# Wide products without a reader in the opening, an earlier first load of modulation tiles, and a fifth raw slot

## The chip, the cores and the metric

The kernel runs on one core of one Trainium2 chip. Its time is the device time of one execution in microseconds (us), from launch to end; the table below gives the median of three runs. The engines are TensorE (PE in the rows; its weight loads are PEld), VectorE (DVE), ScalarE (ACT), GpSimd (POOL) and SyncE (SP), whose queue issues almost all transfers.

## The reference, cut to what matters

Two transformer layers work on a sequence of 512 tokens with 1024 features, in fp32. Each layer modulates a normalised input, projects it, runs four kinds of attention heads side by side, and then a feed-forward block:

```python
c_act = jax.nn.silu(c)
for l in range(DEPTH):
    mod = c_act @ w_ada[l] + b_ada[l]
    sh1, sc1, g1, sh2, sc2, g2 = [t[:, None, :] for t in jnp.split(mod, N_ADA, axis=-1)]
    h = rmsnorm(x, norm_mix_g[l]) * (1.0 + sc1) + sh1
    z = h @ w_in[l]
    ...
    x = x + g1 * (o @ w_out[l])
    h = rmsnorm(x, norm_mlp_g[l]) * (1.0 + sc2) + sh2
    x = x + g2 * (jnp.square(jax.nn.relu(h @ w_up[l])) @ w_down[l])
```

So before the first projection of layer 0 can start, the squares of x must be summed over the features, a reciprocal root taken, and two of the six modulation vectors (the scale, part 1, and the shift, part 0) worked out from 8 MB of `w_ada`.

## The kernel before

Everything lies transposed: features on 128 partitions, eight tiles of features (k = 0 to 7), 512 tokens as columns. A product in fp32 accuracy is made of three products of rounded halves (`hi` and `lo` of the activations, `whi` and `wlo` of the weights). For each weight tile the class `Weights` takes a slot of the pool `rawp` (four slots of 512 KB, given out in turn, shared with later modulation tiles `adaw`), loads it on SP's queue, has ACT copy it to `whi` (L87) and POOL subtract that to `wlo` (two instructions, L91). A slot is free again when both have read it. Nearly all PE work after the opening is such products (`pj`, `px`).

The opening is `start` (L1148). SP's queue issues x (six transfers), two weight tiles, and then in the order of the code one pair of modulation tiles per k (`ada0`, part 1 ahead of part 0, four slots of a pair) with the other weight tiles between. PE first spreads c over all partitions (`cbP`, eight fp32 products of 128 columns). ACT and DVE square and add the eight tiles of x; PE sums the result over the partitions (`nsum`, four products of one column); DVE and POOL make the reciprocal root (`rsv`, `rs`); PE spreads it (`rsb`). For each k DVE then makes the two modulation columns from the pair of tiles (L191, a product with a sum over 1024 columns each) and the normalised tile `ht` (L1196), ACT makes `hi` (L1199), and POOL or DVE `lo`. Five weight tiles (`n` = 5) are worked on at the same time: with each k come three groups of five products (L1223): hi by whi, the earlier lo by whi, and a hi two back by wlo; the last 30 products are a section of their own. That is 120 products in the opening. The banks `pt` of the pool `psT` are two.

The order of instructions on each engine is fixed when the program is built, by a scheduler that works with its own estimate of times; `tc.issue_after` keeps an instruction behind a named one. Each SP transfer carries one of eight completion semaphores in turn (DMAHW0 to DMAHW7 in the rows), so a transfer waits for the one eight places ahead of it to have landed.

After the opening come the projections and heads of layer 0's attention: `mlas` (12 groups of one-column sums), the scores `sc`, ACT's exponentials `e` (L601), POOL's or DVE's scaling of `e` (L573), PE's transposes `pt` (L626), ACT's and DVE's halves `ph` and `pl` of them (L448, L449), and PE's products `po` (L641, L642), with projections of later heads between.

Of the kernel before, what the change touches and what calls it, by code (L numbers as in the profile page):

```python
# [10 lines left out]
F32 = mybir.dt.float32  # L11
# [6 lines left out]
P = 128  # L18
# [4 lines left out]
AHEAD = (1, 3, 2, 1, 0, 0)  # L23
LAHEAD = (2, 3, 2, 1, 0, 0)
PRELOAD = 2
NSPLIT = 3
KPOOL = 5
NJ0 = 1
# [3 lines left out]
NQ = S // P  # L32
# [77 lines left out]
def layer_stack(ctx: ExitStack, tc: tile.TileContext, a, out):  # L110
    nc = tc.nc
    cons = ctx.enter_context(tc.tile_pool(name="cons", bufs=1))
    rawp = ctx.enter_context(tc.tile_pool(name="rawp", bufs=4))
    hlp = ctx.enter_context(tc.tile_pool(name="hlp", bufs=4))
    hsp = ctx.enter_context(tc.tile_pool(name="hsp", bufs=16))
    smp = ctx.enter_context(tc.tile_pool(name="smp", bufs=2))
# [3 lines left out]
    psT = ctx.enter_context(tc.tile_pool(name="psT", bufs=2, space=PSUM))  # L120
# [3 lines left out]
    def mmbank(name):  # L124
        return psA.tile([P, 512], F32, tag="mm", name=name)

    def tmp_tile(name):
        return wkp.tile([P, S], F32, tag="tmp", name=name, bufs=4)
# [3 lines left out]
    X = {}  # L132
# [3 lines left out]
    ident = cons.tile([P, P], F32, name="ident")  # L136
# [15 lines left out]
    def load_consts():  # L152
        nc.sync.dma_start(cs, a["cs"])
        nc.sync.dma_start(maskL, a["maskL"])
        nc.sync.dma_start(cbias, a["cbias"])
        nc.sync.dma_start(cmask, a["cmask"])
        nc.sync.dma_start(bmask, a["bmask"])
        nc.sync.dma_start(csum, a["csum"])

    def load_x(src, queue):  # L160

        v = xp.tile([P, KT // 2, S], F32, tag="V", name="x")
        tiles = [v[:, k, :] for k in range(KT // 2)]
        for k in (0, 2):
            queue.dma_start(v[:, k : k + 2, :], src[:, k : k + 2, :])
        for k in range(KT // 2, KT):
            tiles.append(xp.tile([P, S], F32, tag="KL", name="x", bufs=4))
            queue.dma_start(tiles[k], src[:, k, :])
        X["x"] = tiles
# [3 lines left out]
    cv = vecs[:, OFF_C : OFF_C + KT]  # L173
# [11 lines left out]
    W = Weights(nc, rawp, hlp, 3, 3)  # L185


    def ada_cols(w, l, part, m, cv=cb):

        off = l * VL + OFF_BADA + 8 * part + m  # L190
        last["ada"] = nc.vector.tensor_tensor_reduce(  # L191
            out=w, in0=cv, in1=w, scale=1.0, scalar=vecs[:, off : off + 1],
            op0=ALU.mult, op1=ALU.add, accum_out=mod[l][:, part, m : m + 1],
        )

    def ada_start(pool, m, cv):

        raw = pool.tile([P, 2, 1024], F32, tag="ada0", name="ada0", bufs=4)
        for part in (1, 0):
            nc.sync.dma_start(raw[:, part, :], a["wadaP"][m, :, part, :])  # L200
            ada_cols(raw[:, part, :], 0, part, m, cv)

    ada_todo = [(0, part, m) for part in (2, 4, 3, 5) for m in range(KT)]
    ada_todo += [(1, part, m) for part in (1, 0, 2, 4, 3, 5) for m in range(KT)]
# [1 line left out]
    last = {}  # L206
# [42 lines left out]
    def rstd_cols(ps, n, scale_cols):  # L249

        v = smp.tile([P, 8], F32, tag="rsv", name="rsv")
        for c0, c1, sc in scale_cols:
            nc.vector.tensor_scalar(  # L253
                v[:, c0:c1], ps[:, c0:c1], sc, EPS, op0=ALU.mult, op1=ALU.add
            )
        r = smp.tile([P, 8], F32, tag="rs", name="rs")
        last["pow"] = nc.gpsimd.tensor_tensor(r[:, 0:n], v[:, 0:n], mhalf[:, 0:n], op=ALU.pow)  # L257
        return r

    def bcast_cols(ps, r, c0, n):  # L260

        for j in range(n):
            nc.tensor.matmul(  # L263
                ps[:, j * P : (j + 1) * P],
                r[:, c0 + j : c0 + j + 1].to_broadcast([P, P]), ident,
                start=True, stop=True,
            )

    def sbank(name):
        return psS.tile([P, 512], F32, tag="sc", name=name)  # L270
# [44 lines left out]
    def h_tiles(pool, tag, bufs):  # L315
        return [
            tuple(pool.tile([P, S], F32R, tag=tag, name=f"h{x}", bufs=bufs) for x in ("hi", "lo"))
            for _ in range(KT)
        ]
# [828 lines left out]
    def start(pool, n):  # L1148


        nonlocal psS
        load_x(a["xT"], nc.sync)
        for _ in range(PRELOAD):
            W._load()
        cps = ctx.enter_context(ExitStack())
        psC = cps.enter_context(tc.tile_pool(name="psC", bufs=1, space=PSUM))
        cbP = psC.tile([P, D], F32, name="cbP")
        for k in range(KT):
            nc.tensor.matmul(
                cbP[:, k * P : (k + 1) * P], cact[:, k : k + 1].to_broadcast([P, P]), ident,  # L1160
                start=True, stop=True,
            )
        acc = wkp.tile([P, S], F32, tag="sqacc", name="sqacc", bufs=1)
        nc.scalar.activation(acc, X["x"][0], AF.Square)
        for k in range(1, KT):
            sq = mmbank("sq")
            nc.scalar.activation(sq, X["x"][k], AF.Square)
            nc.vector.tensor_tensor(acc, acc, sq, op=ALU.add)
        rsb = psO.tile([P, 512], F32, tag="po", name="rsb0")
        ps = psT.tile([P, 512], F32, tag="pt", name="nsum")  # L1170
        for j in range(NQ):
            nc.tensor.matmul(
                ps[:, j : j + 1], acc[:, j * P : (j + 1) * P], ones, start=True, stop=True
            )
        r = rstd_cols(ps, NQ, [(0, NQ, 1.0 / D)])
        bcast_cols(rsb, r, 0, NQ)
        hs = h_tiles(hsp, "hs", 16)
        pss = [mmbank("pj") for _ in range(min(n, 3))]
        pss += [psT.tile([P, 512], F32, tag="pt", name="pj") for _ in range(min(n, 5) - 3)]
        W.other_pool.update({i: (pool, 4) for i in range(4)})  # L1180
        ws = []
        gs = smp.tile([P, KT], F32, tag="gs", name="gs")
        for k in range(KT):
            ada_start(pool, k, cbP)
            if k < n:
                W.split_ahead, W.load_ahead = AHEAD[k], LAHEAD[k]
                with tc.issue_after(last["pow"].ins):
                    ws.append(W.get())
            g = vecs[:, OFF_NMIX + k : OFF_NMIX + k + 1]
            nc.scalar.activation(  # L1190
                gs[:, k : k + 1], mod[0][:, 1, k : k + 1], AF.Identity, bias=g, scale=g
            )
            t = tmp_tile("ht")
            hi, lo = hs[k]
            with tc.issue_after(last["ada"].ins):
                last["dve"] = nc.vector.scalar_tensor_tensor(  # L1196
                    t, X["x"][k], gs[:, k : k + 1], rsb, op0=ALU.mult, op1=ALU.mult
                )
            nc.scalar.activation(hi, t, AF.Identity, bias=mod[0][:, 0, k : k + 1])  # L1199
            if k < KPOOL:  # L1200
                nc.scalar.activation(t, t, AF.Identity, bias=mod[0][:, 0, k : k + 1])
                nc.gpsimd.tensor_tensor(lo, t, hi.bitcast(F32), op=ALU.subtract)
            else:
                last["dve"] = nc.vector.scalar_tensor_tensor(
                    lo, t, mod[0][:, 0, k : k + 1], hi.bitcast(F32), op0=ALU.add, op1=ALU.subtract
                )
        for _ in range(NADA):
            i = ada_state["i"]
            raw = pool.tile([P, 2, 1024], F32, tag="ada0", name="ada0", bufs=4)
            nc.sync.dma_start(raw, a["wadaD"][i : i + 2].rearrange("t p r -> p t r"))  # L1210
            with tc.issue_after(last["dve"].ins):
                for j in range(2):
                    ada_cols(raw[:, j, :], *ada_todo[i + j], cbP)
            ada_state["i"] += 2
        W.split_ahead, W.load_ahead = 3, 3
        while W.n_split < n + NSPLIT:
            W._split()
        load_consts()
        nc.scalar.activation(cb, cbP, AF.Copy)
        cps.close()  # L1220
        psS = ctx.enter_context(tc.tile_pool(name="psS", bufs=2, space=PSUM))
        def part(g, w, k, h):
            nc.tensor.matmul(  # L1223
                pss[g], ws[g][w][:, k, :], hs[k][h], start=(k + w + h == 0),
                stop=(k == KT - 1 and w == 1),
            )


        for k in range(KT - 1):
            for w, j, h in ((0, k, 0), (0, k - 1, 1), (1, k - 2, 0)):  # L1230
                if j >= 0:
                    for g in range(n):
                        part(g, w, j, h)
        k = KT - 1
        for g in range(n):
            for w, j, h in (
                (0, k - 1, 1), (1, k - 2, 0), (1, k - 1, 0), (0, k, 0), (0, k, 1), (1, k, 0)
            ):
                part(g, w, j, h)
        return hs, pss  # L1240
# [152 lines left out]
```

## Time and profile before

| | |
|---|---|
| median of 3 runs | 1287.53 us (1287.36 to 1289.71) |
| the profiled execution: its own time | 1289.0 us |
| its span, first to last instruction | 1287.2 us |
| PE busy | 1245.9 us (97% of the span) |
| DVE, ACT, POOL busy | 681.3, 583.4, 545.8 us |
| mean granted clock of TensorE | 0.981 |

The profiled execution lies 1.5 us above the median, and its span 1.8 us below its own time. In the rows a line begins with its start in us and its length; "[3.77 <-POOL e L573]" is the idle time of the engine ahead of it and what ended that. "x5" is the number of instructions merged into a row; an fp32 product of PE is recorded as two. [...]

### The profile page before, as it was taken

To read this page: it belongs to the slowest core of one execution; us is meant where nothing else is said; L and a number is where in the kernel's file an instruction comes from. 1 tells how busy PE (TensorE), PEld (TensorE's weight loads), DVE (VectorE), ACT (ScalarE), POOL (GpSimd) and SP (SyncE) were. 2 spreads that over 40 slices of the span, in tenths; PEclk is the share of its full clock that TensorE was granted. 3 is DMA by queue.
4 is the path that set the end of the run, shared out by engine and by line. 5 is a ranking of instruction groups with operands and counts; after the bars stand their busy time and mean duration, and the time that the engine had idled before them with its cause. 6 is when DMAs were issued, how large, how long until landed. Compare 5 with 4: busy or idle time off the path is not lost. (4 is left out here: it accounts for less than half of the span.)

```text
span 1287.2 us, 17945 instructions
## 1 busy us (share of the span) xinstructions
PE 1245.9 (97%) x6572; PEld 1042.1 (81%) x6572; DVE 681.3 (53%) x1498; ACT 583.4 (45%) x1121; POOL 545.8 (42%) x495
## 2 busy tenths in 40 slices
PE   5989999989999999999999999999999999999997
PEld 4878787879888888888899778778988888888887
DVE  5758867976455554553255685895543223123124
ACT  5557767744442231331245675884443223223120
POOL 5423323454645445445425432334364444444430
PEclk7989999999999999999999999999999999999998
DMA  9645324452366756655334411313142233323312
GB/s 339 246 118 164 115 72 142 148 201 90 120 191 204 243 183 224 222 182 199 126 110 140 135 43 57 99 58 107 50 131 89 93 98 98 98 85 95 99 33 66
DMA packets 53128, 171.02 MB, mean 133 GB/s; under 512 B 6192, under 2 KB 9776, under 8 KB 53040
## 3 DMA queue, kind: packets, MB, share of 16 engines
q1 hardware_dynamic: 51312, 165.67, 39.5%
q10 hardware_dynamic: 1728, 4.20, 1.0%
q8 instruction: 52, 0.85, 0.3%
q14 instruction: 36, 0.29, 0.1%
HBM read 163.29 MB, written 4.19 MB: 130 GB/s over the span
## 5 line engine op out<-in xcount | busy, mean ns | idle before, releaser
L91 POOL TENSOR_TENSOR wlo<-raw,whi 128x512 fp32r<-128x512 f32 (+3 forms) x372 | 488.2, 1337 | 560.8 <-ACT whi L87 525.3
L87 ACT ACTIVATE whi<-raw 128x1024 fp32r<-128x1024 f32 (+3 forms) x186 | 193.8, 1046 | 459.2 <-PE px L368 249.0
L368 PE MATMUL pj<-hlo,whi 128*128 128x512 f32 (+1 forms) x768 | 288.0, 376 | 0.0
L367 PE MATMUL pj<-hhi,whi 128*128 128x512 f32 (+1 forms) x768 | 287.1, 376 | 0.0
L369 PE MATMUL pj<-hhi,wlo 128*128 128x512 f32 (+1 forms) x768 | 287.1, 374 | 0.0
L367 PE MATMUL px<-a,whi 128*128 128x512 f32 (+2 forms) x584 | 214.9, 368 | 0.0
L368 PE MATMUL px<-a,whi 128*128 128x512 f32 (+2 forms) x584 | 214.7, 368 | 0.0
L369 PE MATMUL px<-a,wlo 128*128 128x512 f32 (+2 forms) x584 | 214.6, 368 | 0.0
L411 DVE SCALAR_TENSOR_TENSOR x<-px,mod,x 128x512 f32<-128x512 f32 (+2 forms) x95 | 62.7, 665 | 199.2 <-PE px L369 199.2
L369 PEld LDWEIGHTS pj<-hhi,wlo 128*128 128x128 f32 x768 | 144.9, 189 | 26.7
L368 PEld LDWEIGHTS pj<-hlo,whi 128*128 128x128 f32 x768 | 145.1, 189 | 26.1
L367 PEld LDWEIGHTS pj<-hhi,whi 128*128 128x128 f32 x768 | 144.1, 188 | 26.1
L191 DVE CUSTOM_DVE_ANT_0 adaw<-cb,adaw,vecs 128x1024 f32<-128x1024 f32 x78 | 102.0, 1307 | 50.7 <-DMA adaw<-in_wadaD 50.7
L368 PEld LDWEIGHTS px<-a,whi 128*128 128x128 f32 x584 | 109.7, 188 | 19.7
L367 PEld LDWEIGHTS px<-a,whi 128*128 128x128 f32 x584 | 109.7, 188 | 19.7
L369 PEld LDWEIGHTS px<-a,wlo 128*128 128x128 f32 x584 | 109.7, 188 | 19.7
L1134 DVE SCALAR_TENSOR_TENSOR t<-pj,r 128x512 f32<-128x512 f32 x64 | 44.1, 691 | 148.0 <-ACT r L1133 147.8
L449 DVE TENSOR_TENSOR a<-t,a 128x512 fp32r<-128x512 f32 x64 | 81.8, 1280 | 41.9 <-ACT a L448 41.9
L601 ACT ACTIVATE e<-e,nm 128x128 f32<-128x128 f32 (+5 forms) x160 | 85.9, 539 | 10.3 <-DVE nm L596 9.8
L449 DVE TENSOR_TENSOR pl<-pt,ph 128x512 fp32r<-128x512 f32 (+1 forms) x112 | 64.8, 597 | 5.9 <-ACT ph L448 5.1
L626 PE MATMUL pt<-ident,e 128*128 128x128 f32 x376 | 60.9, 276 | 4.3 <-POOL e L573 3.8
L448 ACT ACTIVATE ph<-pt 128x512 fp32r<-128x512 f32 (+1 forms) x112 | 56.0, 524 | 13.5 <-PE pt L626 12.2
(237 smaller groups left out, 1806.6 us busy)
## 6 DMA issues: line engine op xcount, KB each, us to landing
adaw<-in_wadaD SPq DMA_DIRECT2D x78, 512.0 KB, 4.4
raw<-in_wup SPq DMA_DIRECT2D x64, 512.0 KB, 3.6
raw<-in_wdown SPq DMA_DIRECT2D x64, 512.0 KB, 3.5
raw<-in_winT SPq DMA_DIRECT2D x28, 512.0 KB, 3.8
ada<-in_wadaP SPq DMA_DIRECT2D x16, 512.0 KB, 8.9
raw<-in_wout SPq DMA_DIRECT2D x16, 512.0 KB, 3.5
cw<-in_cw SPq DMA_DIRECT2D x4, 512.0 KB, 5.0
raw<-in_cw SPq DMA_DIRECT2D x4, 512.0 KB, 4.8
```

The source lines that it names most:

```text
L87: self.nc.scalar.activation(vh[0:rows], raw[0:rows], AF.Copy)
L91: eng.tensor_tensor(lo[0:rows, c], flat[0:rows, c], hi[0:rows, c].bitcast(F32), op=ALU.subtract)
L191: last["ada"] = nc.vector.tensor_tensor_reduce(out=w, in0=cv, in1=w, scale=1.0, scalar=vecs[:, off : off + 1], op0=ALU.mult, op1=ALU.add, ...
L367: nc.tensor.matmul(ps, wh[:, k, :], hh[:, c], start=first, stop=False)
L368: nc.tensor.matmul(ps, wh[:, k, :], hl[:, c], start=False, stop=False)
L369: nc.tensor.matmul(ps, wl[:, k, :], hh[:, c], start=False, stop=last)
L411: last["dve"] = nc.vector.scalar_tensor_tensor(X["x"][m][:, c], ps, mod[l][:, part, m : m + 1], X["x"][m][:, c], op0=ALU.mult, op1=ALU.add)
L448: nc.scalar.activation(hi, src, AF.Copy)
L449: last["dve"] = nc.vector.tensor_tensor(lo, src, hi.bitcast(F32), op=ALU.subtract)
L601: nc.scalar.activation(ee, ee, AF.Exp, bias=nm[:, n : n + 1], scale=-1.0, accum_out=den[:, n : n + 1])
L626: nc.tensor.transpose(pt[:, c : c + P], p[n][:, col : col + P], ident)
L1134: nc.vector.scalar_tensor_tensor(t, ps, 0.0, r, op0=ALU.max, op1=ALU.mult)
```

## The change

Six things are edited. `WARM = (7, 2, 3)` gives the numbers of products `warm`: ident by a tile of x, 512 columns, into a bank `pt` that nobody reads. Seven stand on PE behind `cbP`, two behind `nsum`, three behind `rsb`, and `rsb` stands behind the two. `ada_start` now returns the DVE part as a function, so that the first pair of tiles is loaded ahead of the two weight tiles, and the first modulation column on DVE ahead of `rsv`, the second behind it. `rawp` has five slots. The scratch memory that the program keeps for transfers with addresses made on the chip is set to 8192 bytes.

```diff
+WARM = (7, 2, 3)
...
-    rawp = ctx.enter_context(tc.tile_pool(name="rawp", bufs=4))
+    rawp = ctx.enter_context(tc.tile_pool(name="rawp", bufs=5))
...
         for part in (1, 0):
             nc.sync.dma_start(raw[:, part, :], a["wadaP"][m, :, part, :])
-            ada_cols(raw[:, part, :], 0, part, m, cv)
+
+        def products(parts=(1, 0)):
+            for part in parts:
+                ada_cols(raw[:, part, :], 0, part, m, cv)
+        return products
...
         load_x(a["xT"], nc.sync)
-        for _ in range(PRELOAD):
-            W._load()
         cps = ctx.enter_context(ExitStack())
         psC = cps.enter_context(tc.tile_pool(name="psC", bufs=1, space=PSUM))
         cbP = psC.tile([P, D], F32, name="cbP")
+        first = ada_start(pool, 0, cbP)
+        for _ in range(PRELOAD):
+            W._load()
         for k in range(KT):
-            nc.tensor.matmul(
+            w = nc.tensor.matmul(
                 cbP[:, k * P : (k + 1) * P], cact[:, k : k + 1].to_broadcast([P, P]), ident,
                 start=True, stop=True,
             )
+        warm = psT.tile([P, 512], F32, tag="pt", name="warm")
+
+        def keep_warm(ks):
+
+            for k in ks:
+                w = nc.tensor.matmul(warm, ident, X["x"][k], start=True, stop=True)
+            return w
+
+        with tc.issue_after(w.ins):
+            keep_warm(range(WARM[0]))
...
+        with tc.issue_after(w.ins):
+            w = keep_warm(range(WARM[1]))
+        first((1,))
         r = rstd_cols(ps, NQ, [(0, NQ, 1.0 / D)])
-        bcast_cols(rsb, r, 0, NQ)
+        with tc.issue_after(w.ins):
+            w = bcast_cols(rsb, r, 0, NQ)
+        with tc.issue_after(w.ins):
+            keep_warm(range(WARM[2]))
...
         for k in range(KT):
-            ada_start(pool, k, cbP)
+            if k:
+                ada_start(pool, k, cbP)()
+            else:
+                with tc.issue_after(last["rsv"].ins):
+                    first((0,))
...
-    nc = _bacc.Bacc("TRN2", target_bir_lowering=False, num_devices=1)
+    nc = _bacc.Bacc("TRN2", target_bir_lowering=False, num_devices=1, dynamic_dma_scratch_size=8192)
```

On PE, the first instructions of the opening were these:

```order
L1159 MATMUL cbP<-ident,cact 128x128 x8
L1172 MATMUL nsum<-ones,sqacc 128x1 x4
L263 MATMUL rsb_170<-ident,rs 128x128 x4
L1223 MATMUL pj<-hhi,whi_213 128x512
L1223 MATMUL pj<-hhi,whi_218 128x512
```

and now, at the same place, they are these:

```order
L1166 MATMUL cbP<-ident,cact 128x128 x8
L1175 MATMUL warm<-x,ident 128x512 x7
L1189 MATMUL nsum<-ones,sqacc 128x1 x4
L1175 MATMUL warm<-x,ident 128x512 x2
L268 MATMUL rsb_181<-ident,rs 128x128 x4
L1175 MATMUL warm<-x,ident 128x512 x3
L1250 MATMUL pj<-hhi,whi_226 128x512
L1250 MATMUL pj<-hhi,whi_231 128x512
```

Twelve products of 512 columns have come in; nothing else has moved there. On SP's queue, behind the transfers of x, the order was this (`raw` are weight tiles, `ada` modulation tiles; the brackets show the semaphores waited for, DMAHW those of transfers):

```order
L72 DMA raw_131<-in_winT 128x1024 [waits DMAHW0_49]
L72 DMA raw_133<-in_winT 128x1024 [waits DMAHW1_49]
L200 DMA ada_206<-in_wadaP 128x1024 [waits DMAHW2_49]
L200 DMA ada_206<-in_wadaP 128x1024 [waits DMAHW3_49]
L72 DMA raw_211<-in_winT 128x1024 [waits DMAHW4_49]
L200 DMA ada_229<-in_wadaP 128x1024 [waits DMAHW5_49]
L200 DMA ada_229<-in_wadaP 128x1024 [waits DMAHW6_49]
L72 DMA raw_234<-in_winT 128x1024 [waits DMAHW7_49]
L72 DMA raw_236<-in_winT 128x1024 [waits DMAHW0_49,Activation_49,Pool_49]
L200 DMA ada_259<-in_wadaP 128x1024 [waits DMAHW1_49]
```

and is now this:

```order
L201 DMA ada_135<-in_wadaP 128x1024 [waits DMAHW0_49]
L201 DMA ada_135<-in_wadaP 128x1024 [waits DMAHW1_49]
L73 DMA raw_138<-in_winT 128x1024 [waits DMAHW2_49]
L73 DMA raw_140<-in_winT 128x1024 [waits DMAHW3_49]
L73 DMA raw_224<-in_winT 128x1024 [waits DMAHW4_49]
L201 DMA ada_242<-in_wadaP 128x1024 [waits DMAHW5_49]
L201 DMA ada_242<-in_wadaP 128x1024 [waits DMAHW6_49]
L73 DMA raw_247<-in_winT 128x1024 [waits DMAHW7_49]
L73 DMA raw_249<-in_winT 128x1024 [waits DMAHW0_49]
L201 DMA ada_272<-in_wadaP 128x1024 [waits DMAHW1_49]
```

The first pair of modulation tiles has moved ahead of the weights, and the fifth weight tile (`raw_236`, now `raw_249`) no longer waits for ACT and POOL. In the middle of layer 0's attention the scheduler's order has shifted too, on all engines, down to the end of its heads. ACT had this order around the halves `ph` that the first product with the tile `VB` waits for (`whi_2397` is a tile of `w_out`, `kh` and `otmp` belong to other heads):

```order
L601 ACTIVATE e_2328,den<-e_2328,nm 128x128
L87 ACTIVATE whi_2397<-raw_2395 128x1024
L648 ACTIVATE otmp<-po 64x512
L525 ACTIVATE kh<-pj 64x512
L526 ACTIVATE kh<-pj 64x512
L601 ACTIVATE e_2336,den<-e_2336,nm 128x256
L601 ACTIVATE e_2344,den<-e_2344,nm 128x384
L601 ACTIVATE e_2352,den<-e_2352,nm 128x512
L579 ACTIVATE e_2336<-e_2336,rc 128x256
L579 ACTIVATE e_2344<-e_2344,rc 128x384
L448 ACTIVATE ph_2363<-pt 128x512
L448 ACTIVATE ph_2372<-pt 128x512
```

and now has this:

```order
L607 ACTIVATE e_2341,den<-e_2341,nm 128x128
L654 ACTIVATE otmp<-po 64x512
L531 ACTIVATE kh<-pj 64x512
L532 ACTIVATE kh<-pj 64x512
L607 ACTIVATE e_2349,den<-e_2349,nm 128x256
L454 ACTIVATE ph_2376<-pt 128x512
L607 ACTIVATE e_2357,den<-e_2357,nm 128x384
L585 ACTIVATE e_2349<-e_2349,rc 128x256
L454 ACTIVATE ph_2385<-pt 128x512
L585 ACTIVATE e_2357<-e_2357,rc 128x384
L607 ACTIVATE e_2365,den<-e_2365,nm 128x512
L88 ACTIVATE whi_2410<-raw_2408 128x1024
```

The first `ph` has moved up five places and the weight copy down behind all of them. On PE the product `po` that reads it stood behind 17 products `pj` and now stands behind four. From the end of layer 0's heads on, the order on PE, DVE, ACT and POOL is what it was.

## Rows read from the trace of the kernel before

**Rows 1.** The page, parts 1 and 2: busy time; PE's clock in 40 slices.
```profile
PE 1245.9 (97%) x6572; PEld 1042.1 (81%) x6572; DVE 681.3 (53%) x1498; ACT 583.4 (45%) x1121; POOL 545.8 (42%) x495
...
PEclk7989999999999999999999999999999999999998
```
**Rows 2.** Timeline of PE, opening: start us, length us, instructions [idle before <-releaser].
```profile
3.70 3.75 PE L1159 MATMUL cbP<-ident,cact 128*128 128x128 f32 x16 [3.70 <-DVE cact L178]
12.93 1.84 PE L1172 MATMUL nsum<-ones,sqacc 128*128 128x1 f32 x8 [5.47 <-DVE sqacc L1168]
16.19 2.07 PE L263 MATMUL rsb<-ident,rs 128*128 128x128 f32 x8 [1.42 <-POOL rs L257]
19.93 1.65 PE L1223 MATMUL pj<-hhi,whi 128*128 128x512 f32 x3 [1.67 <-ACT hhi L1199]
...
29.57 1.45 PE L1223 MATMUL pj<-hhi,whi 128*128 128x512 f32 x5 [1.48 <-ACT hhi L1199]
...
35.10 1.32 PE L1223 MATMUL pj<-hhi,whi 128*128 128x512 f32 x5
...
55.54 0.39 PE L1223 MATMUL pj<-hhi,wlo 128*128 128x512 f32 x1
```
**Rows 3.** Stretches of the opening: us, busy by engine, PEclk, DMA share, GB/s.
```profile
10.00:11.00 1.00, 0.00 (x0) 0.00 (x0) 0.49 (x1) 0.92 (x2) 0.00 (x0) 0.85 1.05 424
19.00:24.00 5.00, 3.17 (x6) 1.94 (x7) 3.19 (x6) 4.35 (x7) 5.00 (x5) 0.50 0.90 288
28.00:31.00 3.00, 1.52 (x6) 0.86 (x5) 3.00 (x6) 1.72 (x3) 3.00 (x3) 1.00 1.03 412
31.00:35.00 4.00, 3.91 (x11) 3.13 (x11) 4.00 (x9) 1.78 (x4) 2.58 (x3) 0.57 1.02 412
```
**Rows 4.** Timeline of SP's queue, opening.
```profile
11.19 7.77 SPq L72 DMA_DIRECT2D raw<-in_winT  x2
19.00 13.04 SPq L200 DMA_DIRECT2D ada<-in_wadaP  x12
```
**Rows 5.** Timeline of DVE, opening.
```profile
25.07 1.28 DVE L191 CUSTOM_DVE_ANT_0 ada<-cbP,ada,vecs 128x1024 f32<-128x1024 f32 x1 [2.88 <-DMA ada<-in_wadaP]
...
26.81 1.28 DVE L191 CUSTOM_DVE_ANT_0 ada<-cbP,ada,vecs 128x1024 f32<-128x1024 f32 x1 [0.45 <-DMA ada<-in_wadaP]
...
28.02 0.74 DVE L1196 SCALAR_TENSOR_TENSOR ht<-x,gs,rsb 128x512 f32<-128x512 f32 x1
...
44.69 0.75 DVE L1196 SCALAR_TENSOR_TENSOR ht<-x,gs,rsb 128x512 f32<-128x512 f32 x1
```
**Rows 6.** Timelines of PE, POOL, ACT and SP between 72 and 85 us.
```profile
84.22 0.48 PE L626 MATMUL pt<-ident,e 128*128 128x128 f32 x1 [3.77 <-POOL e L573]
...
72.72 0.73 POOL L91 TENSOR_TENSOR wlo<-raw,whi 128x256 fp32r<-128x256 f32 x1
...
81.08 2.49 POOL L91 TENSOR_TENSOR wlo<-raw,whi 128x512 fp32r<-128x512 f32 x2 [5.07 <-ACT whi L87]
...
79.95 1.06 ACT L87 ACTIVATE whi<-raw 128x1024 fp32r<-128x1024 f32 x1 [2.72 <-DMA raw<-in_winT]
...
76.04 0.33 SPq L72 DMA_DIRECT2D raw<-in_winT  x1
```
**Rows 7.** Three stretches of 20 us, columns as in the stretches above.
```profile
80.00:100.00 20.00, 16.23 (x128) 12.48 (x127) 11.91 (x35) 13.41 (x32) 6.14 (x6) 0.83 0.29 83
200.00:220.00 20.00, 17.61 (x88) 14.41 (x87) 12.98 (x38) 14.28 (x33) 5.01 (x7) 0.91 0.47 158
260.00:280.00 20.00, 17.96 (x107) 15.14 (x106) 12.58 (x18) 10.47 (x15) 11.41 (x8) 1.00 0.40 137
```
**Rows 8.** Timelines of PE and ACT at three later waits.
```profile
210.56 0.50 PE L641 MATMUL po<-ph,VB 128*128 128x512 f32 x1 [2.30 <-ACT ph L448]
...
265.98 0.50 PE L367 MATMUL px<-ohi,whi 128*128 128x512 f32 x1 [1.55 <-ACT ohi L448]
...
204.27 1.06 ACT L87 ACTIVATE whi<-raw 128x1024 fp32r<-128x1024 f32 x1 [1.72 <-DMA raw<-in_wout]
```

More of the change, by code (lines that the diff above doesn't have):

```diff
@@ L252, in rstd_cols @@
         for c0, c1, sc in scale_cols:
-            nc.vector.tensor_scalar(
+            last["rsv"] = nc.vector.tensor_scalar(
                 v[:, c0:c1], ps[:, c0:c1], sc, EPS, op0=ALU.mult, op1=ALU.add
@@ L262, in bcast_cols @@
         for j in range(n):
-            nc.tensor.matmul(
+            m = nc.tensor.matmul(
                 ps[:, j * P : (j + 1) * P],
@@ L267, in bcast_cols @@
             )
+        return m
     def sbank(name):
@@ L1157, in start @@
         cbP = psC.tile([P, D], F32, name="cbP")
+        first = ada_start(pool, 0, cbP)
+        for _ in range(PRELOAD):
+            W._load()
         for k in range(KT):
-            nc.tensor.matmul(
+            w = nc.tensor.matmul(
                 cbP[:, k * P : (k + 1) * P], cact[:, k : k + 1].to_broadcast([P, P]), ident,
@@ L1171, in start @@
         for j in range(NQ):
-            nc.tensor.matmul(
+            w = nc.tensor.matmul(
                 ps[:, j : j + 1], acc[:, j * P : (j + 1) * P], ones, start=True, stop=True
             )
+        with tc.issue_after(w.ins):
+            w = keep_warm(range(WARM[1]))
+        first((1,))
         r = rstd_cols(ps, NQ, [(0, NQ, 1.0 / D)])
-        bcast_cols(rsb, r, 0, NQ)
+        with tc.issue_after(w.ins):
+            w = bcast_cols(rsb, r, 0, NQ)
+        with tc.issue_after(w.ins):
+            keep_warm(range(WARM[2]))
         hs = h_tiles(hsp, "hs", 16)
```

## The prediction

> **What bounds the kernel now.** The page comes first: PE is busy for 1245.9 of 1287.2 us [rows 1], so 41.3 us is all that waits cost, and beyond that only a slower clock can be won back. The clock's slices show where it is low: the first is 7, the third 8, all but the last of the others 9 [rows 1]. So I read the timeline of PE in the opening: the waits of 3.70, 5.47, 1.42, 1.67 and 1.48 us there are 13.7 of the 41.3 [rows 2], and the granted clock is 0.50 from 19 to 24 us and 0.57 in the mean from 31 to 35 [rows 3]. After that I looked for other long waits of PE with a low clock behind them: 3.77 us at 84, with a clock of 0.83 over that stretch of 20 us, and 2.30 us at 210, with 0.91 [rows 6 to 8].
>
> What ends last in the opening is read backwards. PE stands until 29.57 for the `hi` of k = 2 [rows 2]; its `ht` begins on DVE at 28.02, behind two modulation columns that waited 2.88 and 0.45 us for their tiles [rows 5]. These tiles were late on SP's queue: two weight issues took 7.77 us there from 11.19 on, and the twelve modulation issues start only at 19.00 [rows 4]. The second of the two needs a slot of `rawp` back. From 28.02 on DVE needs 16.67 us for five k (28.02 to 44.69), 3.3 each [rows 5]; PE needs 15 products for each, and its pace at the high clock is (55.76 - 35.10)/90 = 0.23 us, 90 products lying between 35.10 and the end [rows 2], so 3.4. From there both are near their bounds.
>
> **The change, part by part.** *Seven wide products ahead of `nsum`.* No row of before has an fp32 product of 512 columns. The nearest is `cbP`: eight of 128 columns in 3.75 us, 0.47 each [rows 2]. Four times the columns gives at most 1.9 us, and half that, 0.94, at twice the clock; without the end of the last one, which the 3.75 include, some 0.86. The seven follow `cbP` at 7.45 without a gap. At 0.86 they end at 13.5, 0.6 us behind the 12.93 at which `nsum` started; at 1.9, at 20.7, 7.8 us behind. I take 0.86, because the clock stands at 1.00 until late in the microsecond from 10 on (mean 0.85) though PE has been idle since 7.45 [rows 3]; so it was high by the end of `cbP`, and the products follow that at once. Should it rise late, each product before costs 0.9 more.
>
> *Two and three more.* At the high clock `nsum` takes half of 1.84, so it ends at 14.45. From its end to `rsb` it was 1.42 us [rows 2], and the two products take 1.7, so `rsb` starts at 16.2, as before, and ends 1.0 earlier (half of 2.07). The three end at 19.8, when the first `pj` began before (19.93). Nothing is won or lost by this part itself; at the low clock the five would cost up to 5 x 0.9 = 4.5.
>
> *First modulation column ahead of `rsv`.* It is 1.28 us of DVE [rows 5], ahead of `rsv` and so of `rsb`, while PE is still at the wide products and `nsum`. The tile is now the first transfer behind x, so I take nothing, and 1.3 as the upper end. The weights land that much later, two tiles of 0.52 MB at 0.41 MB/us (412 GB/s [rows 3]), 2.6 us; the first `pj` still needs `rsb` and `ht`.
>
> *The fifth slot, in the opening.* The fifth weight no longer stops the queue. What that brings is bounded by 3.3 us (DVE's two waits [rows 5]) and by nothing. The transfers are one stream, and before the late pair lie the same bytes as before; what can be won is the dip: 288 GB/s from 19 to 24 us against 412 later [rows 3], (412 - 288) x 5 us = 0.62 MB, 1.5 us at 412. I take **-1.5** for all `ht` from k = 2 on: `hi` of k = 2 at 28.1.
>
> *The clock afterwards.* From 29.57 PE had 105 of its 120 products left and took 26.2 us; at 0.23 they are 24.1, so the stretch of 0.57 cost 2.1. Between 19.8 and 28.1 PE still has only 15 products (3.4 us) to do and must wait for `ht`, `lo` and weights; twelve wide products don't fill that. So the low stretch may come again, elsewhere. I take half: **-1.0** (ends 0 and -2.1).
>
> *The fifth slot at 84 us.* PE waits for POOL's `e`, which stands behind two `wlo` (81.08 to 83.57), these behind ACT's `whi` at 79.95, that behind its transfer, issued at 76.04 [rows 6]. Slots go round, so that tile took the slot of the tile four before, which POOL was still subtracting; now it takes the one five before, done at 73.45 [rows 6]. The transfer then lands 2.6 us earlier, and with it `whi`, `wlo` and `e`: the wait shrinks from 3.77 to 1.2. **-2.6** (ends 0, if something else on POOL holds `e`, and -3.77). The clock there: (1 - 0.83) x 20 x 2 = 6.8 us at half [rows 7], of which at most 3.77 are the wait; what was busy lost 1.5 to 3.4 us. A wait of 1.55 us at 265.98 left the clock at 1.00 over its stretch [rows 7, 8], one of 1.48 at 29.57 was followed by 0.57 [rows 2, 3]; 1.2 is below both, so I take it that the clock stays: **-2.2** (ends 0 and -3.4).
>
> *ACT's order at 210 us.* ACT stood 1.72 us for a tile of `w_out` and then copied it for 1.06 [rows 8], all ahead of `ph`. Both now lie behind, with two `e` and two scalings too, so `ph` comes at least 2.8 us earlier; but PE asks for it 13 products, 3.0 us, earlier. If only the 2.8 came, the wait would be 2.5; with the four other instructions (some 0.55 each, as `whi` of half the length) it is about 0.3. I take **-1.5** (ends -2.3 and +0.2); a low clock there, (1 - 0.91) x 20 = 1.8 us lost [rows 7], I leave in, as the lower end. Other places where the order shifted stay at 0, with 1.5 either way.
>
> *The scratch size* touches only transfers that no queue of the profile makes: 0.
>
> The sum is -1.5 - 1.0 - 2.6 - 2.2 - 1.5 = -8.8 us. After the opening all work is released by PE or by what PE released, and PE is 97% busy, so an early start stays early to the end. The profiled execution of 1289.0 would go to 1280.2; it stands 1.5 above the median, so the median goes from 1287.5 to **1278.7**.
>
> **The rivals.** *A: the clock gives nothing back.* Gaps between the new products and the first `pj` leave the low stretches as long as they were, here and at 84 and 210: -1.5 - 2.6 - 1.5 = -5.6, 1281.9. For it: 15 products cannot fill 8.3 us. Against it: the wait at 84 shrinks below any that was followed by a fall in these rows. [...]
>
> *B: the slot is hidden.* POOL holds `e` at 84 for other reasons and DVE's pair comes no earlier; only the clock of the opening and the wait at 210 are won: -2.5, 1285.0, within what a measurement can tell from no change (0.2%, 2.6 us). Against it: both waits name a transfer that waited for a slot.
>
> *C: slower, the wide products hold `nsum`.* If they run at the low clock, `nsum` starts at 20.7 and takes 1.84; two more (3.8) and `rsb` (2.07) end at 28.4, three more (5.6) at 34.0, and 120 products at 0.23 end at 61.6 where 55.76 was: +5.8 in the opening. It decides the sign where it exceeds what the later places give: 1287.5 + 5.8 = 1293.3 if these stay as they are, 1287.0 if they give their 6.3. A rise of the clock after the first four products is about the point from which the opening is no gain. Against it: the clock at 10 us.
>
> *D: the clock gives all*, here, at 84 and at 210: -1.5 - 2.1 - 2.6 - 3.4 - 2.3 - 1.8 = -13.7, 1273.8.
>
> **How the numbers follow.** The forecast (1275.5 to 1281) has 0.47, A 0.23, B 0.11, C 0.10 (0.07 slower, 0.03 about the same), D 0.09. The range goes from D to just beyond B, 1273.8 to 1286.0, and leaves out C and the tails. Faster by more than 0.2% than 1287.5, that is below 1284.9: 0.47 + 0.23 + 0.09 and a part of B, 0.82; within 0.2%: 0.10; slower: 0.08.
>
> **What would show it.** Seven `warm` of some 0.86 us ending near 13.5, `nsum` within a microsecond of 12.9, `rsb` ending at 17.2. Twelve modulation issues no longer starting at 19.00 but spread from 13 us on; DVE's wait of 2.88 down to about 1.5 and `ht` of k = 2 near 26.5; the last `pj` of the opening at 52 to 54. At the transposes that stood at 84.22 a wait of 1.2 and a clock of 1.00 behind it. At the first product with `VB` a wait below 1 us. The prediction is wrong if `nsum` begins after 15, if PE's clock is low for longer than before between 28 and 35, or if new waits of more than 1 us stand between 90 and 210, where the order has shifted.

## The result and the profile after

| | before | after |
|---|---|---|
| median | 1288.62 us (4 runs, 1287.36 to 1290.24) | 1280.76 us (4 runs, 1280.24 to 1281.66) |
| ratio, 95% interval | | 0.9932 [0.9912, 0.9953] |
| the profiled execution: time, span | 1289.0, 1287.2 us | 1280.42, 1278.6 us |
| mean granted clock | 0.981 | 0.993 |

The changed kernel is faster by 7.9 us; 1278.7 was forecast, within 1273.8 to 1286.0. On a second chip, where both were timed again, it was 1283.41 against 1290.51 us (0.9949 [0.9929, 0.9969]), 7.1 us. Single executions of the kernel before lie between 1284.33 and 1295.36 on one chip, so a single execution tells nothing of a few us: below, ratios and medians stand for the time and profiles for the place. The ratios are estimated from all executions; they are no quotients of the medians and differ from these by up to 0.1%. Their intervals, 0.14 to 0.21% either way, are 1.8 to 2.7 us.

The page of the changed kernel, parts 1 and 2 (busy time; PE's clock in 40 slices), beside [rows 1]:

```profile
PE 1247.1 (98%) x6596; PEld 1039.7 (81%) x6596; DVE 681.5 (53%) x1498; ACT 583.5 (46%) x1121; POOL 545.3 (43%) x495
...
PEclk9999999999999999999998999999999999999999
```

PE does the same work and 24 instructions more, twelve wide products of two records each, and the first and third slice of its clock, 7 and 8 before, are now 9. The timeline of PE in the opening (start, length, instructions, idle before and what ended it), beside [rows 2]:

```profile
7.22 6.22 PE L1175 MATMUL warm<-x,ident 128*128 128x512 f32 x14
13.28 0.95 PE L1189 MATMUL nsum<-ones,sqacc 128*128 128x1 f32 x8
14.09 1.96 PE L1175 MATMUL warm<-x,ident 128*128 128x512 f32 x4
15.89 1.05 PE L268 MATMUL rsb<-ident,rs 128*128 128x128 f32 x8
16.78 2.74 PE L1175 MATMUL warm<-x,ident 128*128 128x512 f32 x6
18.96 1.26 PE L1250 MATMUL pj<-hhi,whi 128*128 128x512 f32 x3
22.16 1.81 PE L1250 MATMUL pj<-hhi,whi 128*128 128x512 f32 x5 [1.95 <-ACT whi L88]
...
27.76 1.36 PE L1250 MATMUL pj<-hhi,whi 128*128 128x512 f32 x5
30.84 1.42 PE L1250 MATMUL pj<-hlo,whi 128*128 128x512 f32 x5 [1.71 <-POOL hlo L1229]
...
53.67 0.39 PE L1250 MATMUL pj<-hhi,wlo 128*128 128x512 f32 x1
```

Seven wide products take 6.06 us (7.22 to 13.28), 0.87 each; `nsum` starts 0.35 us later than before, `rsb` ends at 16.94. The four waits of 5.47, 1.42, 1.67 and 1.48 us are gone. The longest two of the new ones are 1.95 us at 22.16, for a weight, and 1.71 at 30.84. The last is released by POOL's `hlo`: `hi` of k = 2 is ready 1.8 us earlier than before, but the products behind it, with the `lo` of k = 1, must wait. The last product of the opening starts at 53.67, where it was 55.54.

Stretches of the changed kernel (us; busy by engine; PEclk, the granted share of the full clock, as a mean over the stretch; DMA share; GB/s), beside [rows 3] and [rows 7]:

```profile
19.00:24.00 5.00, 2.90 (x10) 1.35 (x8) 3.11 (x6) 3.97 (x6) 5.00 (x5) 1.00 1.02 408
24.00:28.00 4.00, 3.39 (x8) 2.50 (x9) 4.00 (x8) 1.76 (x4) 4.00 (x4) 0.57 1.03 409
...
31.00:35.00 4.00, 4.00 (x18) 3.27 (x19) 4.00 (x8) 2.43 (x5) 2.65 (x3) 1.00 1.03 410
80.00:100.00 20.00, 19.48 (x159) 15.34 (x158) 15.82 (x41) 14.34 (x31) 7.32 (x8) 1.00 0.59 194
200.00:220.00 20.00, 19.85 (x101) 15.85 (x100) 17.15 (x42) 13.82 (x30) 9.27 (x6) 1.00 0.51 164
```

The clock is 1.00 where it was 0.50 (19 to 24 us) and 0.57 (31 to 35), and low from 24 to 28 instead (0.57). The dip of the transfers is filled, 408 GB/s against 288. At 80 to 100 and at 200 to 220 us, 0.83 and 0.91 before, it does not fall at all (1.00).

SP's queue and DVE of the changed kernel, beside [rows 4] and [rows 5]:

```profile
10.76 1.64 SPq L73 DMA_DIRECT2D raw<-in_winT  x2
13.36 16.72 SPq L201 DMA_DIRECT2D ada<-in_wadaP  x12
```

```profile
12.33 1.28 DVE L192 CUSTOM_DVE_ANT_0 ada<-cbP,ada,vecs 128x1024 f32<-128x1024 f32 x1
...
14.26 0.16 DVE L258 TENSOR_SCALAR rsv<-nsum 128x4 f32<-128x4 f32 x1 [0.65 <-PE nsum L1189]
...
23.61 1.28 DVE L192 CUSTOM_DVE_ANT_0 ada<-cbP,ada,vecs 128x1024 f32<-128x1024 f32 x1 [1.89 <-DMA ada<-in_wadaP]
...
26.11 0.74 DVE L1223 SCALAR_TENSOR_TENSOR ht<-x,gs,rsb 128x512 f32<-128x512 f32 x1
```

The modulation issues start at 13.36 instead of 19.00, the wait of 2.88 us is 1.89, `ht` of k = 2 starts at 26.11 instead of 28.02. `rsv` is not held by the first modulation column: it waits 0.65 us for `nsum` behind it.

PE's waits after the opening, and the chain ahead of the first (transfer, `whi`, `wlo`), beside [rows 6] and [rows 8]:

```profile
78.21 0.33 PE L632 MATMUL pt<-ident,e 128*128 128x128 f32 x1 [1.10 <-POOL e L579]
...
70.11 0.33 SPq L73 DMA_DIRECT2D raw<-in_winT  x1
...
73.90 1.06 ACT L88 ACTIVATE whi<-raw 128x1024 fp32r<-128x1024 f32 x1
...
75.04 2.52 POOL L92 TENSOR_TENSOR wlo<-raw,whi 128x512 fp32r<-128x512 f32 x2 [2.38 <-ACT whi L88]
...
198.84 0.51 PE L647 MATMUL po<-ph,VB 128*128 128x512 f32 x1 [0.49 <-ACT ph L454]
```

3.77 us has become 1.10, and 2.30 has become 0.49. Measured from the first score product (76.18 before, 72.83 now), the transfer is issued at -2.7 instead of -0.1 us, 2.6 earlier, and ACT no longer waits for it.

**Where the 8.6 us of span came from.** Four starts on PE's timeline cut both profiles: the first `pn`, where the opening ends; the first score product `sc` of the heads; the transposes that wait; and the first product with w_out, `px`.

| stretch | before | after | difference | forecast |
|---|---|---|---|---|
| start to `pn` | 55.76 | 53.90 | -1.9 | -1.5 - 1.0 |
| `pn` to `sc` | 20.42 | 18.93 | -1.5 | 0 |
| `sc` to the transposes | 8.04 | 5.38 | -2.7 | -2.6 |
| transposes to `px` | 139.90 | 135.71 | -4.2 | -2.2 - 1.5 |
| `px` to the end of the span | 1063.1 | 1064.7 | +1.6 | 0 |

The sum is -8.7, for 8.6 from spans that are rounded. The heads gave 6.9 us where 6.3 were forecast. The -1.5 ahead of them and the +1.6 behind were not forecast: at both places the clock falls without a wait of PE next to it (62 to 66 us: 0.59 before, 1.00 after; 672 to 680 after: 0.57, longer than the fall at the same work before, which is 0.57 over the four us from 683 to 687).

### The profile page after: what moved, and what is told of

Its sections match the earlier page's. It is cut to its first block, busy times and chain, and to the rows that moved or that the text cites. A ratio compares the mean times of both kernels' runs of the same rounds, so it can differ in the third digit from the quotient of the medians.

```text
span 1278.6 us, 17988 instructions
## 1 busy us (share of the span) xinstructions
PE 1247.1 (98%) x6596; PEld 1039.7 (81%) x6596; DVE 681.5 (53%) x1498; ACT 583.5 (46%) x1121; POOL 545.3 (43%) x495
```

## The experiments

All were timed against the kernel before on their own chip, in three groups of four. "End" is the start of the first `pn` in us, the next two columns are stretches of the table above.

| kernel | ratio, 95% interval | end | `pn` to `sc` | `sc` to `px` |
|---|---|---|---|---|
| before (first profile) | 1 | 55.76 | 20.42 | 147.94 |
| e4: wide products alone | 1.0019 [1.0003, 1.0034] | 55.25 | 18.94 | 147.94 |
| e2: changed, four slots | 1.0010 [0.9993, 1.0026] | 57.02 | 20.43 | 149.06 |
| e9: changed, fifth slot in the opening only | 1.0016 [1.0002, 1.0030] | 56.25 | 20.44 | 149.79 |
| e1: five slots alone | 0.9950 [0.9929, 0.9970] | 55.40 | 20.44 | 140.94 |
| e3: changed, no wide products | 0.9969 [0.9953, 0.9984] | 58.68 | 18.94 | 140.98 |
| changed, again | 0.9949 [0.9929, 0.9969] | 54.15 | 18.93 | 140.91 |
| e12: wide products and slot | 0.9956 [0.9939, 0.9973] | 56.68 | 20.44 | 141.25 |
| e13: changed, POOL's order swapped | 0.9933 [0.9913, 0.9953] | 51.88 | 20.42 | 140.89 |
| e14: slot and that swap alone | 0.9935 [0.9914, 0.9955] | 51.92 | 20.44 | 141.07 |
| e10: changed, one `hlo` on DVE | 0.9997 [0.9983, 1.0010] | 61.19 | 20.42 | 141.01 |
| e11: changed, twelve ahead of `nsum` | 0.9998 [0.9985, 1.0012] | 62.28 | 18.93 | 141.10 |
| e15: changed, six slots | 0.9958 [0.9945, 0.9972] | 56.01 | 18.93 | 142.35 |

The last column is the main reading. In the four profiles with four slots behind the opening it is 147.9 to 149.8; in the eight experiments with five, and in the changed kernel's first profile (141.09), 140.9 to 141.3, whatever their opening does. The stretch ahead, `pn` to `sc`, is 20.4 us in eight profiles and 18.9 in six. The first is the length with a fall of the clock there: from 62 to 66 us it is 0.59 before (20.42) and 1.00 in the changed kernel (18.93), and in e12, e13 and e14 fourteen or fifteen `pn` in a row take 0.22 us each (the first ones of before 0.12), in e11 and e15 none. (A profile is one execution and need not be near the median: e2 and e9 were profiled at the highest time of their kernel, 1294.4 and 1296.6 us, e4, e15 and the changed kernel again at the lowest, 1286.2, 1280.3 and 1281.4.)

**e1, five slots alone.** `rawp` and the scratch size as in the change, nothing else:

```diff
-    rawp = ctx.enter_context(tc.tile_pool(name="rawp", bufs=4))
+    rawp = ctx.enter_context(tc.tile_pool(name="rawp", bufs=5))
```

> The kernel before with five raw slots and the smaller scratch memory; no wide products, weights loaded first as before. The order on all engines from the heads of layer 0 on is that of the changed kernel. Theory (the slot carries the gain): about -7 us against before (ratio 0.9946), of which -1 in the opening and the rest at the waits formerly at 84 and 210 us with the clock behind them; the opening still has a low clock somewhere between 20 and 35 us. Rival (the wide products carry the clock, and with it half of the gain): -4 us (0.997), with falls of the clock left at 60 to 100 or 200 to 220 us.

0.9950, 6.4 us of 1289.39; the medians alone (1284.48 against 1289.39) give 4.9. It cannot be told from the changed kernel (0.9932 and 0.9949). The wait at the transposes and the clock behind it, and the clock at 200 to 220 us:

```profile
81.10 0.33 PE L626 MATMUL pt<-ident,e 128*128 128x128 f32 x1 [0.99 <-POOL e L573]
...
80.00:100.00 20.00, 18.62 (x155) 14.79 (x155) 15.46 (x40) 14.71 (x33) 7.62 (x9) 1.00 0.50 155
200.00:220.00 20.00, 19.35 (x95) 15.38 (x95) 17.05 (x41) 15.15 (x34) 8.47 (x7) 1.00 0.51 157
```

0.99 us and a clock of 1.00 at both places, without one wide product.

**e4, wide products alone, and e2, the changed kernel with four slots.**

```diff
+WARM = (7, 2, 3)
+        with tc.issue_after(w.ins):
+            keep_warm(range(WARM[0]))
...
```

> The kernel before with only the twelve wide products. Theory (the slot carries the gain): -0.5 us (0 to -1.5), since what PE saves between 31 and 35 us is bounded by the late tiles on DVE; the waits of 3.77 and 2.30 us at 84 and 210 stay. Rival (the wide products carry half of the gain): -3 us or more, with a clock of 1.00 from 60 to 100 us.

> The changed kernel with four raw slots; wide products and early load stay. The order from the heads of layer 0 on is that of the kernel before. Theory: the waits at about 84 and 210 us are back with some 3.8 and 2.3 us, so -1 us against before (ratio 0.999), +7 over the changed kernel; in the opening DVE waits some 3 us for the pair of k = 2 again. Rival (wide products): -4 us against before (0.997).

Neither is faster than before, so the rival is out; e4 is slower by 0.2%, 2.4 us (0.4 to 4.4), where the theory had 0 to -1.5. Both e2 and e9 below have the smaller scratch memory with four slots, so it is not what gains. The waits are back, 4.03 and 2.37 us in e4, 4.08 and 2.51 in e2.

**e3, the changed kernel without wide products.**

```diff
-        with tc.issue_after(w.ins):
-            keep_warm(range(WARM[0]))
...
```

> The changed kernel without its twelve wide products; slot and early load stay. Theory: +0.5 us over the changed kernel (0 to +1.5), so -7.5 against before (ratio 0.994); the opening ends at 54 to 55.5 us. Rival: +3 us or more over the changed kernel, -5 against before (0.996).

By its number this is the rival's case: 0.9969, and an opening that ends at 58.68. But the scheduler turned more than that: POOL now has six `wlo`, not four, between the first `hlo` and the second, and PE waits 3.02 us for the second. As a test of the wide products it is confounded; e13 and e14, further down, compare kernels with and without them under one order of POOL.

**e9, the fifth slot in the opening only.**

```diff
-    rawp = ctx.enter_context(tc.tile_pool(name="rawp", bufs=5))
+    rawp = ctx.enter_context(tc.tile_pool(name="rawp", bufs=4))
...
+        if i == 4:
+            raw = self.fifth.tile([P, 1024], F32, tag="raw4", name=f"raw{i}", bufs=1)
```

> The changed kernel with the fifth slot in the opening only: the fifth weight tile of the opening lies in the opening's own pool, and rawp has four slots after it; the order behind the opening is that of before. Theory (the slot's worth lies behind the opening): the opening ends near 53.9 as in the changed kernel, the waits of about 4.0 and 2.4 us at the transposes and at the first product with VB are back: -2 us against before (0.9985), +6 over the changed kernel. Rival (the opening's transfers carry the gain): within 2 us of the changed kernel.

1.0016: all of the gain is gone, even the -2 that I gave the opening. Timeline and windows of e9 at the two places:

```profile
85.35 0.48 PE L635 MATMUL pt<-ident,e 128*128 128x128 f32 x1 [4.38 <-POOL e L582]
...
212.98 0.80 PE L650 MATMUL po<-ph,VB 128*128 128x512 f32 x1 [2.45 <-ACT ph L457]
...
86.00:90.00 4.00, 4.00 (x16) 3.36 (x15) 1.23 (x6) 0.80 (x3) 0.02 (x1) 0.51 0.48 159
213.00:217.00 4.00, 4.00 (x15) 3.44 (x15) 2.67 (x4) 1.07 (x3) 0.00 (x0) 0.60 0.77 282
```

Waits of 4.38 and 2.45 us, with a clock of 0.51 and 0.60 behind them.

**The changed kernel again, and e12, slot and wide products with the weights loaded first as before.** Against the changed kernel e12 differs by this, and the first pair's two columns stand together on DVE:

```diff
-        first = ada_start(pool, 0, cbP)
...
         for k in range(KT):
-            if k:
-                ada_start(pool, k, cbP)()
...
+            ada_start(pool, k, cbP)
```

> The changed kernel itself, on the chip of the runs beside it. Both theories: -6 to -9 us against before (0.993 to 0.995). If it is the slot that makes nearly all of it, it stands level with the slot alone (0.995); if the twelve wide products add 2 us or more to the slot, it stands at 0.9935 or lower.

> Wide products and slot, but the weights loaded ahead of the first pair of modulation tiles, as before. Theory (POOL's chain of ten wlo and two hlo, which starts behind rs, sets when PE gets the hlo of k = 1): rsv waits behind the first modulation column, rs starts at 16.1 and not 14.6, so the hlo of k = 1 comes 1.5 us later and the opening ends at 55.4 instead of 53.9; the rest as in the changed kernel; +1.5 over it. Rival (the early load delays the weights, and these set the pace): the opening ends at 53 or earlier, -1 against the changed kernel.

The changed kernel stands level with the slot alone (0.9949 and 0.9950, on two chips), so the wide products add nothing that can be told; an effect of 2 to 3 us could hide in the intervals. In e12 `rs` starts at 15.99 instead of 14.58, the `hlo` of k = 1 lets PE go at 32.05 instead of 30.84, as POOL's chain says; the clock is then low from 32 to 36 us (0.57), in spite of the wide products, and the end is 56.68, not 55.4. The ratio of e12 (0.9956) is too near the changed kernel's to tell the 1.5 us.

**e10, the `hlo` of k = 1 on DVE.**

```diff
-            if k < KPOOL:
+            if k < KPOOL and k != 1:
```

> The changed kernel with the hlo of k = 1 on DVE, which stands idle for 1.89 us ahead of the pair of k = 2, instead of on POOL. Theory (POOL's chain): the wait of 1.71 us at 30.8 goes, the opening ends at 52.2; -1.7 against the changed kernel. Rival (the tiles of k = 3 or the weights are late at the same point): the wait is then for hhi or wlo, less than 0.5 us gained.

Neither came true: 0.9997, no gain at all. DVE, POOL and PE of e10:

```profile
22.54 8.20 DVE L1231 SCALAR_TENSOR_TENSOR hlo<-ht,mod,hhi 128x512 fp32r<-128x512 f32 x1 [0.79 <-ACT hhi L1226]
...
16.45 7.56 POOL L92 TENSOR_TENSOR wlo<-raw,whi 128x512 fp32r<-128x512 f32 x6
23.95 1.28 POOL L1229 TENSOR_TENSOR hlo<-ht,hhi 128x512 fp32r<-128x512 f32 x1
25.17 5.02 POOL L92 TENSOR_TENSOR wlo<-raw,whi 128x512 fp32r<-128x512 f32 x4
...
34.61 2.50 PE L1250 MATMUL pj<-hhi,whi 128*128 128x512 f32 x5 [7.44 <-ACT hhi L1226]
```

The same operation takes 0.74 us on DVE at 37.17 in the changed kernel, while POOL stands. Here it took 8.20, to 30.74, just behind the end of POOL's unbroken row of `wlo` and `hlo` at 30.19; all modulation columns stood behind it, and PE waited 7.44 us.

**e13, the `hlo` of k = 1 ahead of the last four `wlo` on POOL, and e14, the same on the slot alone.**

```diff
+            if i in self.defer:
+                self.late.append(low)
+            else:
+                low()
...
+                if k == 1:
+                    with tc.issue_after(lw.ins):
+                        for low in W.late:
+                            low()
```

(`low` is the pair of `wlo` instructions, `defer` the fourth and fifth weight, `lw` the `hlo`.)

> The changed kernel with one thing swapped on POOL: the hlo of k = 1 stands ahead of the four wlo of the fourth and fifth weight, not behind them. Theory (POOL's chain sets the end of the opening): that hlo is done at 25.8 and not at 30.8, PE's wait of 1.7 us there goes, and the late wlo, done at 30.8, still come in time; the opening ends at 52.2, -1.7 us against the changed kernel. Rival (the next thing is late at the same point): a wait of PE for wlo or hhi between 28 and 33 takes its place, and less than 0.5 us is won.

> The kernel before with five slots and POOL's swapped order, without wide products and without the early load. Theory (the wide products are worth nothing that lasts): the opening ends at 55.4 - 1.7 = 53.7 and the kernel is level with the same order under the wide products, within 1.5 us. Rival (they hold the clock, and only POOL's wait hid that): clock at 0.50 again between 30 and 36 us, the opening ends at 55 or later, 2 us or more slower than with them.

POOL and PE of e13:

```profile
23.16 2.53 POOL L1237 TENSOR_TENSOR hlo<-ht,hhi 128x512 fp32r<-128x512 f32 x2
25.64 5.08 POOL L94 TENSOR_TENSOR wlo<-raw,whi 128x512 fp32r<-128x512 f32 x4
...
28.95 1.31 PE L1262 MATMUL pj<-hlo,whi 128*128 128x512 f32 x5
```

The wait is gone, nothing takes its place, and the opening ends at 51.88, 2.0 us earlier. Windows and PE of e14, which has no wide product:

```profile
10.00:20.00 10.00, 4.30 (x17) 3.95 (x18) 6.66 (x13) 5.73 (x8) 5.21 (x5) 0.52 1.03 401
20.00:27.00 7.00, 6.03 (x14) 3.87 (x14) 5.17 (x10) 4.25 (x8) 7.00 (x7) 0.50 1.03 414
28.00:36.00 8.00, 8.00 (x36) 6.53 (x36) 8.00 (x15) 4.17 (x8) 6.56 (x6) 1.00 1.03 410
...
29.00 1.31 PE L1235 MATMUL pj<-hlo,whi 128*128 128x512 f32 x5
```

Its clock is 0.52 in the mean from 10 to 20 us and 0.50 from there to 27, and its opening ends at 51.92, where the theory had 53.7: the fall from 31 to 35 us that e1 has (0.57) did not come either. With ratios of 0.9935 and 0.9933 on the same chip (1281.69 and 1281.03 us against 1289.84), no worth of the wide products and the early load can be told here, and in the profiles the slow clock ahead of 27 us costs nothing. Both ratios are below the changed kernel's on its second chip (0.9949), but level with that on its first (0.9932), and the intervals overlap; that the opening is 2 us shorter is shown by the profile only.

**e11, twelve wide products ahead of `nsum`.**

```diff
-WARM = (7, 2, 3)
+WARM = (12, 2, 3)
```

> The changed kernel with twelve wide products ahead of nsum instead of seven: nsum, rsv, rs and rsb come 5 x 0.87 = 4.3 us later. Theory (POOL's chain starts behind rs): every wlo and hlo moves with it, the hlo of k = 1 ends at 35, the opening ends at 58: +4 us over the changed kernel. Rival (DVE waits for the tiles of k = 2 anyway, and these set the end): ht of k = 2 moves from 26.1 to 27.8, the opening ends at 55.6: +1.7.

POOL and PE of e11:

```profile
20.76 12.49 POOL L92 TENSOR_TENSOR wlo<-raw,whi 128x512 fp32r<-128x512 f32 x10
33.21 5.00 POOL L1229 TENSOR_TENSOR hlo<-ht,hhi 128x512 fp32r<-128x512 f32 x4
...
34.53 2.50 PE L1250 MATMUL pj<-hlo,whi 128*128 128x512 f32 x5 [6.83 <-POOL hlo L1229]
```

`nsum` comes at 18.49 instead of 13.28, and the opening ends at 62.28: +8.4, twice what POOL's chain alone gives, far from the rival's +1.7. The scheduler put all ten `wlo` ahead of both `hlo`, and behind the wait of 6.83 us five products take 2.50 us, where five take 1.31 at 28.95 in e13.

**e15, six slots.**

```diff
-    rawp = ctx.enter_context(tc.tile_pool(name="rawp", bufs=5))
+    rawp = ctx.enter_context(tc.tile_pool(name="rawp", bufs=6))
```

> The changed kernel with a sixth raw slot (the room comes from a still smaller scratch memory). Theory (with five slots no transfer that PE waits for waits for a slot): level with the changed kernel within 1.5 us; the wait of 1.1 us at the transposes, released by POOL's scaling of e behind two wlo, stays; the order in the heads of layer 0 shifts once more. Rival (slots still hold transfers back): -2 us or more, with that wait below 0.5 us.

0.9958: no gain over five slots. The wait at the transposes did not stay at 1.1 us, as the theory had it, but is 2.05, behind POOL's `e` and, ahead of that, ACT's `whi`, which stands 0.97 us for its transfer again. Why that transfer is late with six slots stays open.

## Why the prediction was right, and where it was not

**The fifth slot at 84 us** was right in mechanism and size: 3.77 to 1.10 us, -2.7 against -2.6. The transfer is issued 2.6 us earlier, as worked out, and the order of ACT and POOL around the wait is the one of before, so it is the slot that counts here. What is left of the wait is POOL's own: its two `wlo` end at 77.56 and `e` behind them at 78.16. The four-slot kernels keep the wait (3.8 to 4.4), the five-slot ones don't (1.0 to 1.2).

**The clock there** was right too, and Rival A with it refuted in the heads. The clock fell behind both waits before (0.83 and 0.91 over 20 us) and in e9 (0.51 and 0.60 just behind them), with four slots there; with five it was 1.00 over both stretches in the changed kernel and in e1. A product `po` at 148.80 before and 140.74 now divides the stretch from the transposes to `px`. Ahead of it PE does the same work 2.05 us sooner, against -2.2; that part takes 62.45 to 62.56 us in all nine profiles with five slots and 63.86 to 65.35 in the four with four. Behind it the stretch lost 2.1 us, against -1.5 for **ACT's order**: the wait itself fell by 1.8 (2.30 to 0.49), but PE's idle time in this part by about 1 only, and its busy time by 1.2 (72.06 to 70.87), because the clock at 210 rose too (0.91 to 1.00 over 200 to 220 us), which the sum had left out. There the new order comes with the slot, and no run has one without the other. Of the waits that are new between 90 and 210 us none is longer than 0.56. Ahead of `sc` the fall comes and goes without a pattern over the kernels of the table: that stretch is 18.9 or 20.4 us. In the heads the falls come and go with the wait: there with waits of 3.77 and 2.30 us before and 4.38 and 2.45 in e9, absent with 1.10 and 0.49 in the changed kernel. The wait of 1.10 us left the clock at 1.00, as the wait of 1.55 at 265.98 had (1.00 from 260 to 280 us [rows 7, 8]).

**The opening** is where the working failed. The step is "What ends last in the opening": it follows DVE's `ht` to the `hi` of k = 2, and takes the 1.5 us of earlier transfers through to PE. They arrived (`ht` 1.9 us earlier, the queue as forecast), but PE did not gain from them. POOL in the opening before and after (start, length):

```profile
16.09 7.50 POOL L91 TENSOR_TENSOR wlo<-raw,whi 128x512 fp32r<-128x512 f32 x6
...
24.78 5.03 POOL L91 TENSOR_TENSOR wlo<-raw,whi 128x512 fp32r<-128x512 f32 x4
29.77 2.53 POOL L1202 TENSOR_TENSOR hlo<-ht,hhi 128x512 fp32r<-128x512 f32 x2
```

```profile
14.58 1.02 POOL L262 TENSOR_TENSOR rs<-rsv,mhalf 128x4 f32<-128x4 f32 x1 [13.58 <-DVE rsv L258]
15.79 7.52 POOL L92 TENSOR_TENSOR wlo<-raw,whi 128x512 fp32r<-128x512 f32 x6 [0.19 <-ACT whi L88]
23.27 1.29 POOL L1229 TENSOR_TENSOR hlo<-ht,hhi 128x512 fp32r<-128x512 f32 x1
24.51 5.04 POOL L92 TENSOR_TENSOR wlo<-raw,whi 128x512 fp32r<-128x512 f32 x4
29.49 3.79 POOL L1229 TENSOR_TENSOR hlo<-ht,hhi 128x512 fp32r<-128x512 f32 x3
```

Ten `wlo` of 1.25 us and the `hlo` of k = 0 and 1 stand in one unbroken row behind `rs`; the second `hlo` ends at some 31.0 us before (29.77 + half of 2.53) and 30.8 after (29.49 + a third of 3.79). Before, PE asks for it at 29.57 + 5 x 0.23 = 30.7 and starts on it at 31.12, so it hid: two chains ended together, and I read one. Moving one gave a wait of 1.71 us on the other. POOL's row starts at 16.09 before and 15.79 after, behind `rs`, so that earlier tiles for k = 2 do not move it; e12, e13 and e11 move its start or its order, and PE's wait and the end follow, with falls of the clock or a new order on top.

What the opening did give in the profile is -1.9. From this `hlo` to `pn` PE took 24.64 us before (31.12 to 55.76) and 23.06 after (30.84 to 53.90): 1.6 us are the low clock behind 31 us (0.57 before, 1.00 after; 2.1 in the working, of which I took half, -1.0), and 0.3 are POOL's earlier row. Both profiles of the changed kernel show it, but it is no property of the wide products: e9, e12 and e15 have them and a clock of 0.58, 0.57 and 0.59 from 32 to 36 us, and e14, without them, has 1.00 from 28 on. What decides on this fall stays open. **The wide products themselves** cost what was said, 0.87 against 0.86, and `rsb` 16.94 against 17.2; that they bring nothing that can be told fits the waits behind them: PE stands 1.95 and 1.71 us for ACT and POOL there in any case. Rival C's late `nsum` was not seen; in e11, where it comes 5.2 us late, the opening ends 8.4 us later, with a new order on POOL besides. **The first modulation column** ahead of `rsv` cost nothing, as taken, but only since its pair is loaded first: in e12 `rsv` is 1.4 us later (15.68 against 14.26).

So the total was right with two wrong parts: the heads gave 6.9 us, not 6.3, and do so in every five-slot profile; the opening gave 1.9 for other reasons than transfers and, by ratios, nothing that can be told (e4 and e2 with a part of its change and e9 with all of it, none with the slot behind it, are no faster than before). That the -1.5 and +1.6 around the heads, which were not forecast, cancel is luck. What stays open is what makes the clock fall ahead of `sc`, and why the two chips differ by 0.8 us in the gain, less than their intervals.

## What to carry to other kernels

Before a late tile is moved, list every engine that feeds the stalled one and where each chain ends: a second chain that ends within a few tenths of a microsecond takes the whole gain (here 1.71 us on POOL). An engine in order, like POOL here, may be helped by the order of its row: in the profiles one swap gave 2.0 us where twelve products and an early load gave nothing that could be told. The slow clock of e14 (0.50 from 20 to 27 us) cost nothing where PE had to wait for other engines in any case; look first whether it does, and measure one part of a change at a time.

## What the runs showed of the hardware that was not expected

DVE's `hlo`, with two operands in SBUF, took 8.20 us beside a busy POOL (e10, at 22.54) and 0.74 beside an idle one (the changed kernel, at 37.17), while `ht` (its third operand, `rsb`, lies in PSUM) took 0.74 beside the same busy POOL (e10, at 21.01). In e10 it lasted not for one instruction of POOL's but from 22.54 to 30.74, past the end of POOL's row at 30.19, beside at least six instructions back to back. What holds it there, and whether it is the place of the operands that tells the two apart, durations do not show.

A clock of 0.52 in the mean from 10 to 20 us and 0.50 from there to 27 (e14, whose `nsum` and `rsb` take 1.84 and 2.07 us) and one at which these take 0.95 and 1.05 (e13) gave openings that end at 51.92 and 51.88.
